# Grouped-query attention: row sums of the probabilities from a column of ones in the value matmuls, in place of running sums on POOL

## The chip, the cores and the metric

The kernel runs on one core of a Trainium2 chip. The metric is the device time of one execution in microseconds. The engines are named as in the profile: PE is the matrix engine (PEld its loads of weights), DVE the vector engine, ACT the scalar engine, POOL the general-purpose engine, SP the engine that issues most DMAs.

## The reference, cut to what matters

The program is a two-layer backbone over 1024 latent tokens and 256 context tokens of width 1024. The change lies in the even layer's mixer, where one half of the width is grouped-query attention: 8 query heads of 64 share 2 key and value heads. Latent queries attend to all 1280 tokens, context queries to the 256 of the context. The part that is computed differently is the softmax and what is multiplied with the values:

```python
def gqa_attend(q, keys, vals):
    ...
    def one(qblk):
        s = jnp.einsum('bqkgd,bskd->bkgqs', qblk, keys).astype(jnp.float32) * hd ** -0.5
        pr = jax.nn.softmax(s, axis=-1).astype(vals.dtype)
        return jnp.einsum('bkgqs,bskd->bqkgd', pr, vals)
```

## The kernel before

The kernel holds a float32 number as two parts, `hi` (rounded to the matrix engine's fast 32-bit form) and `lo` (what is left), made by `split`: ACT writes `hi` as a copy (L94), DVE writes `lo` as a subtraction (L95). A product is then two or three matmuls that add up in PSUM.

**The projection stage** (`in_proj0`, about 40 to 300 us). For each of the 10 token tiles of 128 (2 of context, 8 latent) `prep_kv` takes the projected keys and values. The values of the two heads are split into `v_st` (128 tokens, 2 heads, `hi` and `lo` of 64 columns) and stored by a DMA on SP to `gv` in DRAM (L505). `v_st` has one buffer. Then come the norm of the keys (`hr_ss`, `rs_t`), their rotation (`rp_u`, `rp_o`) and, one or two steps later, the transposes `kt_ps` on PE. Beside this runs `ada_halves`, which multiplies modulation weights (`w_ada`) on DVE into `ada_acc`.

**The attention stage** (`gqa`, about 300 to 668 us). A unit is one tile of 128 queries and one key head, hence 4 query heads, 512 columns side by side. There are 16 units of latent tiles, each over 10 key blocks of 128 tokens, and 4 of context tiles, each over 2: 168 key blocks in all. One unit's maxima are found while the unit before is computed: `score` (L731) makes scores by query rows, DVE reduces them to `gq_mx` (L732), then to `gq_m` and the negated `gq_mr` (L737), and `maxima` turns these into a row of 512 by four small matmuls `m_ps` (L743). For each key block, `front` makes the transposed scores `st_ps` with two matmuls (L751, L752; the second carries the maxima as an extra row), ACT takes the exponential into `gq_p` (L754), and `split` makes `gq_hi` and `gq_lo`. POOL adds `gq_p` into a running sum `gq_acc` for the unit: nothing at the first key block, L762 at the second, L765 at each further one. Two steps later `back` multiplies with the values: the weights are the 64 `hi` and 64 `lo` columns of the value head, and two matmuls with `gq_hi` (L772) and `gq_lo` (L773) as moving data add into `o_ps`. Rows 0 to 63 of `o_ps` then hold the product with the `hi` values, rows 64 to 127 that with the `lo` values.

At a unit's end `out` copies `o_ps` to SBUF (`o_sb`, L778) and `finish` takes the row sums: four transposes of `gq_acc` on PE (`l_ps`, L788, in one of the two PSUM banks that the scores `st_ps` use), a reduction of the 128 key rows on DVE (`gq_rl`, L789) and a reciprocal (L790). Four transposes of `o_sb` (`ot_ps`, L798) bring the result back to query rows, ACT and DVE add the two halves (L800, L801), and DVE scales by the reciprocal (L802).

The stages of one key block are written one behind the other, and `pipelined` interleaves successive blocks. `weave` mixes in `side0`, other work in fixed proportion: the remaining projection columns (`vg_ps`, L680 to L682, until about 625 us) and then the Hyena filters of the next layer (`tap_ps`, `hy_h`). On top of the written order a scheduler places the instructions of each engine by its own estimate of readiness; each engine then runs its row in that order.

Of the kernel before, what the change touches and what calls it, by code (L numbers as in the profile page):

```python
# [8 lines left out]
F32 = mybir.dt.float32  # L9
FR = mybir.dt.float32r  # L10
U32 = mybir.dt.uint32
ACTF = mybir.ActivationFunctionType
ALU = mybir.AluOpType
AX = mybir.AxisListType
# [9 lines left out]
NT = NC_T + NX_T  # L24
# [12 lines left out]
def f(ap):  # L37
    return ap.bitcast(F32)
# [43 lines left out]
def psa(g, shape, dt=F32, name="pa", tag="tr"):  # L82
    if tag not in g.ps_bufs:
        tag = "ac" if tag == "hy" and 0 and "ac" in g.ps_bufs else "sx"
    return g.ps.tile(shape, dt, name=name, tag=tag, bufs=g.ps_bufs[tag])
# [6 lines left out]
def split(g, hi, lo, src, pool=False):  # L92

    g.nc.scalar.activation(hi, src, ACTF.Copy)  # L94
    (g.nc.gpsimd if pool else g.nc.vector).tensor_tensor(lo, src, f(hi), op=ALU.subtract)  # L95
# [369 lines left out]
def in_proj0(g, ps, ftp, vgp):  # L465

    nc = g.nc
    src = (g.i["ctx"][0], g.i["x"][0])  # L470
    g.p0 = [g.dram.tile([128, GQA_Q], F32, name=f"p0_{t}") for t in range(NT)]
    g.gq = [g.dram.tile([128, 8, 128], F32, name=f"gq_{t}") for t in range(NT)]
    g.gk = g.dram.tile([128, 4, NT * 128], F32, name="gk")
    g.gv = g.dram.tile([128, NT, 256], F32, name="gv")
    w = g.i["ev_w_in"][0]
    ft = FeatT(g, ftp, ftp.tile([128, KT, 2, 256], FR, name="ftc", tag="ftc"))
    with ExitStack() as st:
        stg = st.enter_context(g.tc.tile_pool(name="ip_stg", bufs=3, reuse_waits="tile"))
        pr = st.enter_context(g.tc.tile_pool(name="ip_pr", bufs=1, reuse_waits="tile"))
        pq = []  # L480

        def head_norm(src, nh, gain):
            r = head_rstd(g, pq[0], src, nh, 64, f"rp_u{nh}")
            nc.vector.tensor_tensor(src, src, r.unsqueeze(2).to_broadcast([128, nh, 64]), op=ALU.mult)
            nc.gpsimd.tensor_tensor(src, src, gain.unsqueeze(1).to_broadcast([128, nh, 64]), op=ALU.mult)
# [13 lines left out]
        def prep_kv(t, ps):  # L499
            st = pq[0].tile([128, 288], F32, name="stg", tag="stgq", bufs=3)  # L500
            nc.scalar.copy(st, ps)
            nc.scalar.dma_start(out=g.p0[t][:, 1536:1568], in_=st[:, 0:32])
            vs = pq[0].tile([128, 2, 2, 64], FR, name="v_st", tag="v_st")
            split(g, vs[:, :, 0, :], vs[:, :, 1, :], st[:, 160:288].rearrange("p (h d) -> p h d", d=64))
            nc.sync.dma_start(out=g.gv[:, t, :], in_=f(vs).rearrange("p h w d -> p (h w d)"))  # L505
            src = st[:, 32:160].rearrange("p (h d) -> p h d", d=64)
            head_norm(src, 2, gk)
            return t, src
# [183 lines left out]
def gqa(g, y_put):  # L692


    nc = g.nc
    with ExitStack() as st:
        kv = st.enter_context(g.tc.tile_pool(name="gq_kv", bufs=1, reuse_waits="tile"))
        pr = st.enter_context(g.tc.tile_pool(name="gq_pr", bufs=2, reuse_waits="tile"))
        units = [(t, h) for t in range(NC_T, NT) for h in range(2)]
        ctx_units = [(t, h) for t in range(NC_T) for h in range(2)]  # L700
        qs, mx, sums, outs = {}, {}, {}, {}

        def load_q(u):
            t, h = u
# [5 lines left out]

        k1 = kv.tile([128, 2, NT * 128], FR, name="gq_k1")
        k2 = kv.tile([65, 2, NT * 128], FR, name="gq_k2")
        v = kv.tile([128, NT, 2, 2, 64], FR, name="gq_v")
        gk = g.gk.rearrange("p (h w) t -> p h w t", w=2)
        nc.sync.dma_start(out=f(k1), in_=gk[:, :, 0, :])
        load_q(units[0])
# [1 line left out]
        ones = kv.tile([128, 1], F32, name="gq_one")  # L718
        nc.vector.memset(ones, 1.0)
        for h in range(2):  # L720
            nc.vector.tensor_copy(k2[64:65, h, :], ones[64:65].to_broadcast([1, NT * 128]))
        nc.sync.dma_start(out=f(v).rearrange("p t h w d -> p t (h w d)"), in_=g.gv)

        def score(u, i):
            t, h = u
# [20 lines left out]
        def front(u, kt, nk):  # L746
            h = u[1]
            q1, q2 = (x.rearrange("p a b -> p (a b)") for x in qs[u])
            ks = slice(kt * 128, kt * 128 + 128)
            ps = psa(g, [128, 512], name="st_ps", tag="sk")  # L750
            nc.tensor.matmul(ps, k1[:, h, ks], q1, start=True, stop=False)  # L751
            nc.tensor.matmul(ps, k2[:, h, ks], q2, start=False, stop=True)  # L752
            p = pr.tile([128, 512], F32, name="gq_p", bufs=3)
            nc.scalar.activation(p, ps, ACTF.Exp, scale=0.125)  # L754
            hi = pr.tile([128, 512], FR, name="gq_hi", bufs=2 + 1)
            lo = pr.tile([128, 512], FR, name="gq_lo", bufs=2 + 1)
            split(g, hi, lo, p)
            if kt == 0:
                sums[u] = p
            elif kt == 1:  # L760
                acc = pr.tile([128, 512], F32, name="gq_acc")
                nc.gpsimd.tensor_tensor(acc, sums[u], p, op=ALU.add)  # L762
                sums[u] = acc
            else:
                nc.gpsimd.tensor_tensor(sums[u], sums[u], p, op=ALU.add)  # L765
            return u, kt, nk, hi, lo

        def back(u, kt, nk, hi, lo):
            if kt == 0:
                outs[u] = psa(g, [128, 512], name="o_ps", tag="o")  # L770
            vl = v[:, kt, u[1]].rearrange("p a d -> p (a d)")
            nc.tensor.matmul(outs[u], vl, hi, start=(kt == 0), stop=False)  # L772
            nc.tensor.matmul(outs[u], vl, lo, start=False, stop=(kt == nk - 1))  # L773
            return u,

# [4 lines left out]

        def finish(u, o_sb):
            t, h = u
            acc = sums.pop(u)
            rl = g.small.tile([128, 4], F32, name="gq_rl")
            if 1:
                ps = psa(g, [128, 4, 128], name="l_ps", tag=["tr", "ac", "sk", "sx"][2])
                for i in range(4):
                    nc.tensor.transpose(ps[:, i, :], acc[:, i * 128:(i + 1) * 128], g.ident)  # L788
                nc.vector.tensor_reduce(rl, ps, axis=AX.X, op=ALU.add)  # L789
                nc.vector.reciprocal(rl, rl)  # L790
            else:
                ps = psa(g, [128, 4], name="l_ps")
                for i in range(4):
                    nc.tensor.matmul(ps[:, i:i + 1], acc[:, i * 128:(i + 1) * 128], ones, start=True, stop=True)
                nc.vector.reciprocal(rl, ps)
            ps = psa(g, [128, 4, 128], name="ot_ps")
            for i in range(4):
                nc.tensor.transpose(ps[:, i, :], o_sb[:, i * 128:(i + 1) * 128], g.ident)  # L798
            y = pr.tile([128, 2, 4, 64], F32, name="gq_y")
            nc.scalar.copy(y[:, 0], ps[:, :, 64:128])  # L800
            nc.vector.tensor_tensor(y[:, 0], ps[:, :, 0:64], y[:, 0], op=ALU.add)  # L801
            nc.vector.tensor_tensor(y[:, 1], y[:, 0], rl.unsqueeze(2).to_broadcast([128, 4, 64]), op=ALU.mult)  # L802
            y_put(t, h * 256, y[:, 1].rearrange("p h d -> p (h d)"))

        def item(u, kt, nk):
# [1579 lines left out]
def tile_kernel(ctx, tc, ins, out):  # L2385
# [17 lines left out]
    with ExitStack() as sp:  # L2403
        banks(g, sp, "ps_d0", tr=2, ac=2, pb=2)
        hy_hidden(g)
        vg = in_proj0(g, sp, ftp, lambda: pool_of(s0, "vg", "right"))
# [195 lines left out]
```

## Time and profile before

| | |
|---|---|
| three runs, median (lowest to highest) | 3425.45 us (3423.26 to 3429.85) |
| the profiled execution's own time | 3425.51 us |
| its span in the trace | 3423.7 us |
| granted clock of PE over the span | 0.962 |
| busy, share of the span: PE, PEld | 91%, 70% |
| busy, share of the span: DVE, ACT, POOL | 75%, 45%, 22% |
| instructions on POOL over the span | 540 |

The span is what the trace covers; the 1.8 us between it and the execution's own time lie around it. PE's busy share counts each matmul from its start to its modelled end, and matmuls overlap, so a busy PE need not be one that takes a new matmul as soon as it could. A wait names the instruction whose end released the one that waited.

### The profile page before, as it was taken

How to read it: one execution, taken by the hardware profiler on the slowest of the kernel's cores; microseconds unless marked ns; L12 is line 12 of the kernel's file. 1: busy time of each engine (PE TensorE's matmuls, PEld its weight loads, DVE VectorE, ACT ScalarE, POOL GpSimd, SP SyncE). 2: the span in 40 equal slices, each digit the busy share in tenths (PEclk: the TensorE clock that was granted, in tenths of full speed). 3: DMA queues.
4: the chain of work that ended last, by engine and by line, in shares of the span. 5: the costliest groups of instructions: out<-in, count | busy, mean ns of one | idle time of the engine just before them, and what ended most of it. 6: DMA issues, size and time to landing. Idle time of an engine off the chain costs nothing.

```text
span 3423.7 us, 42030 instructions
## 1 busy us (share of the span) xinstructions
PE 3129.8 (91%) x13808; PEld 2402.8 (70%) x13808; DVE 2570.6 (75%) x4506; ACT 1538.5 (45%) x3150; POOL 736.5 (22%) x540
## 2 busy tenths in 40 slices
PE   8878999888987999989998899999968989999998
PEld 4765677567765788878877677776634667887886
DVE  6788898968748767666778757577788489876777
ACT  4444666645556222223345543576621352224443
POOL 0254555523322122200110112100011112210000
PEclk9999999899998999999999899999989999999999
DMA  6534111477753433468767445533344635438964
GB/s 227 152 122 148 48 44 44 117 221 212 259 201 110 142 133 132 148 218 298 255 227 230 167 151 166 131 88 77 125 133 147 209 112 183 142 139 296 313 197 156
DMA packets 344583, 566.69 MB, mean 166 GB/s; under 512 B 43329, under 2 KB 138561, under 8 KB 344236
## 3 DMA queue, kind: packets, MB, share of 16 engines
q1 hardware_dynamic: 296244, 491.17, 44.0%
q10 hardware_dynamic: 40952, 47.67, 4.1%
q0 software_dynamic: 7168, 25.17, 2.6%
q8 instruction: 109, 1.79, 0.2%
q14 instruction: 110, 0.90, 0.1%
HBM read 410.35 MB, written 153.54 MB: 165 GB/s over the span
## 4 chain that ended last, share of the span: by engine, by line
PE 56%; DVE 21%; issue 8%; DMA 7%; ACT 4%; POOL 3%; SPq 0%; ACTq 0%; POOLq 0%; DVEq 0%
PE up_ps L105 5%; PE up_ps L104 5%; PE up_ps L103 5%; PE dn_ps L1527 5%; PE dn_ps L1526 5%; PE dn_ps L1528 5%; DVE gq_lo L95 2%; DVE gq_mx L732 2%; PE s_ps L637 2%; PE up_ps L1245 1%; PE o_ps L2235 1%; DVE ada_acc L261 1%; DMA dn_b<-in_w_mlp_out 1%; PE pj_ps L104 1%; PE pj_ps L103 1%
## 5 line engine op out<-in xcount | busy, mean ns | idle before, releaser
L1526 PE MATMUL dn_ps<-dn_w_hi,dn_h_hi 128*128 128x512 f32 x896 | 352.9, 396 | 30.4 <-DVE accy L1507 16.1
L1527 PE MATMUL dn_ps<-dn_w_lo,dn_h_hi 128*128 128x512 f32 x896 | 354.1, 395 | 5.7 <-DVE dn_w_lo L95 5.5
L1528 PE MATMUL dn_ps<-dn_w_hi,dn_h_lo 128*128 128x512 f32 x896 | 352.7, 394 | 0.0
L95 POOL TENSOR_TENSOR w_lo<-up_w,w_hi 128x512 fp32r<-128x512 f32 x106 | 146.1, 1388 | 582.9 <-ACT w_hi L94 582.8
L94 ACT ACTIVATE dn_h_hi<-dn_h 128x512 fp32r<-128x512 f32 x224 | 140.8, 629 | 278.5 <-PE dn_ps L1527 196.4
L95 DVE TENSOR_TENSOR dn_h_lo<-dn_h,dn_h_hi 128x512 fp32r<-128x512 f32 x224 | 161.7, 722 | 79.7 <-ACT dn_h_hi L94 79.3
L1526 PEld LDWEIGHTS dn_ps<-dn_w_hi,dn_h_hi 128*128 128x128 f32 x896 | 170.4, 190 | 70.5 <-DVE accy L1507 17.7
L765 POOL TENSOR_TENSOR gq_acc<-gq_acc,gq_p 128x512 f32<-128x512 f32 x128 | 183.7, 1435 | 88.8 <-ACT gq_p L754 85.5
L1527 PEld LDWEIGHTS dn_ps<-dn_w_lo,dn_h_hi 128*128 128x128 f32 x896 | 171.0, 191 | 45.2 <-DVE dn_w_lo L95 9.8
L1528 PEld LDWEIGHTS dn_ps<-dn_w_hi,dn_h_lo 128*128 128x128 f32 x896 | 170.7, 190 | 35.5
L95 DVE TENSOR_TENSOR gq_lo<-gq_p,gq_hi 128x512 fp32r<-128x512 f32 x168 | 176.0, 1059 | 19.8 <-ACT gq_hi L94 19.5
L261 DVE SCALAR_TENSOR_TENSOR ada_acc<-w_ada,sc,ada_acc 128x512 f32<-128x512 f32 x224 | 170.6, 799 | 22.3 <-DMA w_ada<-in_w_ada 21.6
L95 POOL TENSOR_TENSOR ada_hl<-ada_acc,ada_hl 128x512 fp32r<-128x512 f32 x32 | 64.0, 2013 | 514.2 <-ACT ada_hl L94 362.5
L94 ACT ACTIVATE s_hi<-up_w 128x512 fp32r<-128x512 f32 x128 | 79.3, 630 | 190.4 <-DVE up_w L1234 116.3
L105 PE MATMUL up_ps<-t_hi,s_lo 128*128 128x512 f32 x384 | 152.7, 399 | 2.6 <-DVE s_lo L95 2.6
L104 PE MATMUL up_ps<-t_lo,s_hi 128*128 128x512 f32 x384 | 152.7, 398 | 1.9 <-DVE t_lo L95 1.9
L103 PE MATMUL up_ps<-t_hi,s_hi 128*128 128x512 f32 x384 | 153.1, 399 | 1.4 <-ACT t_hi L94 1.3
L1234 DVE TENSOR_TENSOR up_w<-up_w 128x512 f32<-128x512 f32 x128 | 94.0, 737 | 78.7 <-POOL w_lo L95 76.9
L647 DVE TENSOR_REDUCE sm_m<-s_ps 128x1 f32<-128x512 f32 (+1 forms) x192 | 110.5, 597 | 45.6 <-PE s_ps L637 44.3
L754 ACT ACTIVATE gq_p<-st_ps 128x512 f32<-128x512 f32 x168 | 99.5, 596 | 74.3 <-PE st_ps L752 57.0
L661 ACT ACTIVATE df_p<-s_ps,sm_m 128x512 f32<-128x512 f32 (+1 forms) x192 | 116.8, 619 | 34.5 <-DVE sm_m L651 31.2
L94 ACT ACTIVATE w_hi<-up_w 128x512 fp32r<-128x512 f32 x106 | 64.7, 629 | 145.1 <-DMA up_w<-in_w_mlp_in 65.1
(500 smaller groups left out, 9033.5 us busy)
## 6 DMA issues: line engine op xcount, KB each, us to landing
dn_b<-in_w_mlp_out SPq DMA_DIRECT2D x252, 256.0 KB
w_ada<-in_w_ada SPq DMA_DIRECT2D x96, 512.0 KB
up_w<-in_w_mlp_in SPq DMA_DIRECT2D x32, 1024.0 KB
hy_m<-in_k_ff POOLq DMA_DIRECT2D x32, 512.0 KB, 5.1
dn_c<-hidc SPq DMA_DIRECT2D x64, 256.0 KB
x<-x_in SPq DMA_DIRECT2D x26, 512.0 KB
x_in<-x SPq DMA_DIRECT2D x26, 512.0 KB
cb_raw<-in_od_w_in SPq DMA_DIRECT2D x20, 512.0 KB
```

The lines of the kernel that those rows point to most:

```text
L94: g.nc.scalar.activation(hi, src, ACTF.Copy)
L95: (g.nc.gpsimd if pool else g.nc.vector).tensor_tensor(lo, src, f(hi), op=ALU.subtract)
L103: nc.tensor.matmul(out, ah, bh, start=(i == 0), stop=False)
L104: nc.tensor.matmul(out, ah, bl, start=False, stop=False)
L105: nc.tensor.matmul(out, al, bh, start=False, stop=(i == n - 1))
L261: nc.vector.scalar_tensor_tensor(acc[:, s], w[:, k], sc, acc[:, s], op0=ALU.mult, op1=ALU.add)
L647: nc.vector.tensor_reduce(m[:, i:i + 1], s, axis=AX.X, op=ALU.max)
L661: g.nc.scalar.activation(d, s, ACTF.Exp, bias=m, scale=0.125, accum_out=l[:, i:i + 1])
L765: nc.gpsimd.tensor_tensor(sums[u], sums[u], p, op=ALU.add)
L1526: nc.tensor.matmul(ps, hh[:, sl], wh, start=(k == 0), stop=False)
L1527: nc.tensor.matmul(ps, hh[:, sl], wl, start=False, stop=False)
L1528: nc.tensor.matmul(ps, hl[:, sl], wh, start=False, stop=(k == nb - 1))
```

## The change

In the projection, `v_st` becomes 129 columns for each head: the 64 `hi` columns, one column of ones, the `lo` parts of columns 1 to 63, and last the `lo` part of column 0. The split becomes the copy on ACT, two subtractions and one copy of ones on DVE. `gv` and `gq_v` hold 258 numbers per token in place of 256.

In the attention the matmuls of `back` take columns 0 to 127 as weights. Row 64 of `o_ps` then sums the probabilities themselves. The missing `lo` column 0 gets a matmul of its own for each key block, with one column of weights and `gq_hi` as moving data, which adds into row 0 of `o_ps`. The additions on POOL, the transposes `l_ps` and the reduction L789 are gone; the reciprocal is taken from column 64 of the transposed result, and the addition of the halves covers columns 1 to 63.

```diff
-    g.gv = g.dram.tile([128, NT, 256], F32, name="gv")
+    g.gv = g.dram.tile([128, NT, 258], F32, name="gv")
...
+        ones = pr.tile([128, 1, 1], F32, name="v_one")
+        nc.vector.memset(ones, 1.0)
...
-            vs = pq[0].tile([128, 2, 2, 64], FR, name="v_st", tag="v_st")
-            split(g, vs[:, :, 0, :], vs[:, :, 1, :], st[:, 160:288].rearrange("p (h d) -> p h d", d=64))
-            nc.sync.dma_start(out=g.gv[:, t, :], in_=f(vs).rearrange("p h w d -> p (h w d)"))
+            vs = pq[0].tile([128, 2, 129], FR, name="v_st", tag="v_st")
+            vr = st[:, 160:288].rearrange("p (h d) -> p h d", d=64)
+            nc.scalar.activation(vs[:, :, 0:64], vr, ACTF.Copy)
+            for d0, d1, c0 in ((1, 64, 65), (0, 1, 128)):
+                nc.vector.tensor_tensor(vs[:, :, c0:c0 + d1 - d0], vr[:, :, d0:d1], f(vs[:, :, d0:d1]), op=ALU.subtract)
+            nc.vector.tensor_copy(vs[:, :, 64:65], ones.to_broadcast([128, 2, 1]))
+            nc.sync.dma_start(out=g.gv[:, t, :], in_=f(vs).rearrange("p h d -> p (h d)"))
...
-        v = kv.tile([128, NT, 2, 2, 64], FR, name="gq_v")
+        v = kv.tile([128, NT, 2, 129], FR, name="gq_v")
...
-            if kt == 0:
-                sums[u] = p
-            elif kt == 1:
-                acc = pr.tile([128, 512], F32, name="gq_acc")
-                nc.gpsimd.tensor_tensor(acc, sums[u], p, op=ALU.add)
-                sums[u] = acc
-            else:
-                nc.gpsimd.tensor_tensor(sums[u], sums[u], p, op=ALU.add)
...
-            vl = v[:, kt, u[1]].rearrange("p a d -> p (a d)")
+            vl = v[:, kt, u[1], 0:128]
             nc.tensor.matmul(outs[u], vl, hi, start=(kt == 0), stop=False)
+            nc.tensor.matmul(outs[u][0:1], v[:, kt, u[1], 128:129], hi, start=False, stop=False)
             nc.tensor.matmul(outs[u], vl, lo, start=False, stop=(kt == nk - 1))
...
-                for i in range(4):
-                    nc.tensor.transpose(ps[:, i, :], acc[:, i * 128:(i + 1) * 128], g.ident)
-                nc.vector.tensor_reduce(rl, ps, axis=AX.X, op=ALU.add)
-                nc.vector.reciprocal(rl, rl)
...
-            nc.scalar.copy(y[:, 0], ps[:, :, 64:128])
-            nc.vector.tensor_tensor(y[:, 0], ps[:, :, 0:64], y[:, 0], op=ALU.add)
-            nc.vector.tensor_tensor(y[:, 1], y[:, 0], rl.unsqueeze(2).to_broadcast([128, 4, 64]), op=ALU.mult)
+            nc.vector.reciprocal(rl, ps[:, :, 64:65])
+            nc.scalar.copy(y[:, 0], ps[:, :, 0:64])
+            nc.vector.tensor_tensor(y[:, 0, :, 1:64], ps[:, :, 65:128], y[:, 0, :, 1:64], op=ALU.add)
+            nc.vector.tensor_tensor(y[:, 1], y[:, 0], rl.to_broadcast([128, 4, 64]), op=ALU.mult)
```

Because a scheduler places the instructions, their order changes with the edit, from the value split to shortly behind the attention stage; before and behind that the rows of PE are the same. Three places follow, each as it stands in the two programs. Names with a number are buffers (`q_5149` is a query tile of the unit, `q_5432` one of the next).

PE, at the end of a latent unit in the middle of the stage, before: each key block has two value matmuls, and at the unit's end stand the two sets of four transposes.

```order
L751 MATMUL st_ps<-q_5149,gq_k_2721 128x512
L752 MATMUL st_ps<-q_5150,gq_k_2722 128x512
L772 MATMUL o_ps<-gq_hi,gq_v 128x512
L773 MATMUL o_ps<-gq_lo,gq_v 128x512
L788 MATMUL l_ps<-ident,gq_acc 128x128 x4
L798 MATMUL ot_ps<-ident,o_sb 128x128 x4
L751 MATMUL st_ps<-q_5149,gq_k_2721 128x512
L752 MATMUL st_ps<-q_5150,gq_k_2722 128x512
L772 MATMUL o_ps<-gq_hi,gq_v 128x512
L773 MATMUL o_ps<-gq_lo,gq_v 128x512
```

And after, at the corresponding place (line numbers shift by a few):

```order
L758 MATMUL st_ps<-q_5103,gq_k_2743 128x512
L759 MATMUL st_ps<-q_5104,gq_k_2744 128x512
L771 MATMUL o_ps<-gq_hi,gq_v 128x512
L772 MATMUL o_ps<-gq_hi,gq_v 1x512
L773 MATMUL o_ps<-gq_lo,gq_v 128x512
L786 MATMUL ot_ps<-ident,o_sb 128x128 x4
L758 MATMUL st_ps<-q_5103,gq_k_2743 128x512
L759 MATMUL st_ps<-q_5104,gq_k_2744 128x512
L771 MATMUL o_ps<-gq_hi,gq_v 128x512
L772 MATMUL o_ps<-gq_hi,gq_v 1x512
L773 MATMUL o_ps<-gq_lo,gq_v 128x512
```

One set of transposes is gone, and each key block has a third matmul, 1x512, between the `gq_hi` and the `gq_lo` one.

POOL, at the passage from the projection to the attention, before (`ada_hl` belongs to the modulation, `rp_u` and `rp_o` to the rotation of queries):

```order
L609 TENSOR_TENSOR rp_u<-stg,tq_328 128x256 x2
L611 TENSOR_TENSOR rp_o<-rp_o,rp_u 128x512
L95 TENSOR_TENSOR ada_hl<-ada_acc,ada_hl 128x512 x2
L762 TENSOR_TENSOR gq_acc<-gq_p 128x512
L765 TENSOR_TENSOR gq_acc<-gq_acc,gq_p 128x512 x8
```

And after (`qblk`, `vblk` and `ab` are buffers of the stage behind the attention, set to zero):

```order
L616 TENSOR_TENSOR rp_u<-stg,tq_330 128x256 x2
L618 TENSOR_TENSOR rp_o<-rp_o,rp_u 128x512
L95 TENSOR_TENSOR ada_hl<-ada_acc,ada_hl 128x512 x2
L875 MEMSET qblk_6590 128x1024
L875 MEMSET vblk_6591 128x1024
L875 MEMSET ab_6592 128x1024
```

Between the last work of the projection and the buffers of the next stage POOL has nothing left to do.

DVE, in the projection around one tile's value split, before:

```order
L118 SCALAR_TENSOR_TENSOR rs_t<-rs_t 128x2
L261 SCALAR_TENSOR_TENSOR ada_acc<-w_ada,sc,ada_acc 128x512
L484 TENSOR_TENSOR stg<-stg,rs_t 128x128
L95 TENSOR_TENSOR v_st<-stg,v_st 128x2x64
L113 TENSOR_SCALAR rs_t<-hr_ss 128x2
L604 TENSOR_TENSOR rp_o<-stg,tq_327 128x128
L261 SCALAR_TENSOR_TENSOR ada_acc<-w_ada,sc,ada_acc 128x512 x2
L116 SCALAR_TENSOR_TENSOR rs_t<-rs_t 128x2
```

And after:

```order
L261 SCALAR_TENSOR_TENSOR ada_acc<-w_ada,sc,ada_acc 128x512
L511 CAST v_st<-v_one 128x2
L116 SCALAR_TENSOR_TENSOR rs_t<-rs_t 128x2
L510 TENSOR_TENSOR v_st<-stg,v_st 128x2x63
L510 TENSOR_TENSOR v_st<-stg,v_st 128x2
L117 TENSOR_TENSOR rs_t<-rs_t 128x2
L261 SCALAR_TENSOR_TENSOR ada_acc<-w_ada,sc,ada_acc 128x512
L118 SCALAR_TENSOR_TENSOR rs_t<-rs_t 128x2
L261 SCALAR_TENSOR_TENSOR ada_acc<-w_ada,sc,ada_acc 128x512
L487 TENSOR_TENSOR stg<-stg,rs_t 128x128
L261 SCALAR_TENSOR_TENSOR ada_acc<-w_ada,sc,ada_acc 128x512
```

One row on `v_st` has become three, spread between the norm of the keys and the `ada_acc` operations. On SP, two of the ten stores of `v_st` also stand one `w_ada` load later than before.

## Rows read from the trace of the kernel before

**Rows 1.** Windows: stretch, length, busy per engine (instructions), PE's granted clock, DMA share, GB/s.
```profile
309.00:668.00 359.00, 321.31 (x1442) 240.67 (x1441) 329.86 (x501) 239.31 (x419) 217.28 (x157) 0.97 0.17 53
120.00:290.00 170.00, 136.83 (x698) 110.00 (x697) 137.94 (x275) 68.28 (x176) 83.90 (x80) 0.91 0.50 154
...
418.30:441.40 23.10, 19.63 (x85) 13.53 (x84) 22.32 (x33) 15.22 (x28) 15.37 (x10) 1.00 0.07 23
...
576.20:597.10 20.90, 20.34 (x96) 16.08 (x95) 19.65 (x30) 13.95 (x26) 12.78 (x9) 1.00 0.12 39
...
645.60:666.20 20.60, 15.38 (x55) 9.53 (x53) 20.57 (x26) 12.41 (x25) 12.31 (x8) 0.84 0.35 96
...
632.30:635.70 3.40, 3.14 (x11) 2.59 (x12) 3.40 (x9) 2.20 (x4) 3.40 (x4) 0.50 0.05 10
639.10:642.50 3.40, 3.30 (x9) 2.57 (x10) 3.29 (x7) 2.80 (x6) 2.08 (x3) 0.51 1.01 260
659.60:669.90 10.30, 8.21 (x21) 5.29 (x22) 9.08 (x14) 3.35 (x6) 3.48 (x3) 0.50 0.20 59
```

**Rows 2.** Waits of PE from 309 to 668: total us, times, longest.
```profile
PE o_ps L773 <- DVE gq_lo L95: 18.3, 28, 1.9
PE m_ps L743 <- DVE gq_mr L737: 11.5, 12, 2.0
PE s_ps L731 <- DVE gq_mx L732: 2.3, 3, 0.9
PE m_ps L743 <- DVE gq_mx L732: 1.8, 1, 1.8
PE tap_ps L1905 <- DVE w_lo L95: 1.3, 1, 1.3
PE st_ps L751 <- DVE gq_rl L789: 0.9, 1, 0.9
```

**Rows 3.** Timeline of PE at a unit's end: start, us, instruction.
```profile
490.53 0.39 PE L773 MATMUL o_ps<-gq_lo,gq_v 128*128 128x512 f32 x1
...
490.76 0.60 PE L788 MATMUL l_ps<-ident,gq_acc 128*128 128x128 f32 x4
...
491.20 0.60 PE L798 MATMUL ot_ps<-ident,o_sb 128*128 128x128 f32 x4
```

**Rows 4.** Page, costliest groups: busy us, mean ns, idle before and releaser.
```profile
L95 DVE TENSOR_TENSOR dn_h_lo<-dn_h,dn_h_hi 128x512 fp32r<-128x512 f32 x224 | 161.7, 722 | 79.7 <-ACT dn_h_hi L94 79.3
...
L95 DVE TENSOR_TENSOR gq_lo<-gq_p,gq_hi 128x512 fp32r<-128x512 f32 x168 | 176.0, 1059 | 19.8 <-ACT gq_hi L94 19.5
```

**Rows 5.** Timeline of POOL and DVE in the attention stage.
```profile
483.90 1.28 POOL L765 TENSOR_TENSOR gq_acc<-gq_acc,gq_p 128x512 f32<-128x512 f32 x1 [1.95 <-ACT gq_p L754]
...
484.45 1.28 DVE L95 TENSOR_TENSOR gq_lo<-gq_p,gq_hi 128x512 fp32r<-128x512 f32 x1 [1.89 <-ACT gq_hi L94]
...
486.67 0.68 DVE L95 TENSOR_TENSOR gq_lo<-gq_p,gq_hi 128x512 fp32r<-128x512 f32 x1
```

**Rows 6.** Groups by line, 309 to 668: busy us, mean ns, idle before.
```profile
L789 DVE TENSOR_REDUCE gq_rl<-l_ps 128x4 f32<-128x512 f32 x20 | 13.6, 678 | 0.3 <-PE l_ps L788 0.3
...
L737 DVE TENSOR_SCALAR gq_mr<-gq_m 128x4 fp32r<-128x4 f32 x19 | 12.4, 654 | 0.3
```

**Rows 7.** Groups by line, 120 to 180, DVE in the projection.
```profile
L95 DVE TENSOR_TENSOR v_st<-stg,v_st 128x128 fp32r<-128x128 f32 x10 | 3.3, 326 | 1.6 <-ACT v_st L94 1.6
...
L118 DVE SCALAR_TENSOR_TENSOR rs_t<-rs_t 128x2 f32<-128x2 f32 x9 | 1.4, 153 | 0.0
```

**Rows 8.** Timeline of PE and PEld around one-column matmuls of the modulation rows.
```profile
1767.29 0.39 PE L1539 MATMUL dc_ps<-dx_hi,dn_c 128*128 128x512 f32 x1
...
1767.52 0.63 PE L277 MATMUL ada_ps<-ada_hl,colsr 128*1 128x512 f32 x2
...
1767.75 0.19 PEld L1526 LDWEIGHTS dn_ps<-dn_w_hi,dn_h_hi 128*128 128x128 f32 x1 [0.15 <-issue]
...
1767.99 0.39 PE L1526 MATMUL dn_ps<-dn_w_hi,dn_h_hi 128*128 128x512 f32 x1
```

More of the change, by code (lines that the diff above doesn't have):

```diff
@@ L700, in gqa @@
         ctx_units = [(t, h) for t in range(NC_T) for h in range(2)]
-        qs, mx, sums, outs = {}, {}, {}, {}
+        qs, mx, outs = {}, {}, {}
         def load_q(u):
@@ L721, in gqa @@
             nc.vector.tensor_copy(k2[64:65, h, :], ones[64:65].to_broadcast([1, NT * 128]))
-        nc.sync.dma_start(out=f(v).rearrange("p t h w d -> p t (h w d)"), in_=g.gv)
+        nc.sync.dma_start(out=f(v).rearrange("p t h d -> p t (h d)"), in_=g.gv)
         def score(u, i):
@@ L782, in finish @@
             t, h = u
[L783 to L786, printed above, removed]
-                for i in range(4):
-                    nc.tensor.transpose(ps[:, i, :], acc[:, i * 128:(i + 1) * 128], g.ident)
-                nc.vector.tensor_reduce(rl, ps, axis=AX.X, op=ALU.add)
-                nc.vector.reciprocal(rl, rl)
[L791 to L795, printed above, removed]
+            rl = g.small.tile([128, 4, 1], F32, name="gq_rl")
             ps = psa(g, [128, 4, 128], name="ot_ps")
```

## The prediction

> **What bounds the kernel now.** I read the windows first, one for the whole attention stage (309 to 668 us) and one for each of its units, then the waits of PE, the timeline where two engines meet, and the groups by line.
>
> The stage is 359 us long; PE is busy for 321.31 of it, DVE for 329.86, ACT for 239.31, POOL for 217.28 [rows 1]. So two engines are close to full, and which of them sets the pace changes from unit to unit. In the unit from 418.3 to 441.4 DVE works 22.32 of 23.10 us and PE only 19.63; in the last unit DVE works 20.57 of 20.60 and PE 15.38; in the unit from 576.2 to 597.1 PE works 20.34 of 20.90 [rows 1]. The waits of PE say the same: it stood 18.3 us in 28 places for `gq_lo`, 11.5 and 1.8 us in 13 places for the maxima, and 2.3, 1.3 and 0.9 us in 5 more for other results of DVE [rows 2]. That is 36.1 us in 46 gaps, all behind DVE. A matmul lasts 0.39 us but the next starts 0.23 us behind it [rows 3], so each gap hides another 0.16 us of an array that drains and still counts as busy: 46 x 0.16 = 7.4 us. PE thus loses 43.5 us to DVE, say 45 with the gaps too short to be seen.
>
> Why DVE is full is in two more views. The 168 `gq_lo` subtractions average 1059 ns; the same operation on the same shape in the down projection averages 722 [rows 4]. The timeline shows the mechanism: a POOL addition runs from 483.90 to 485.18; a `gq_lo` that starts under it at 484.45 takes 1.28 us, which is 0.73 until POOL has ended and 0.55 behind that; the next one, with POOL idle, takes 0.68 [rows 5]. While POOL adds, DVE's subtraction of two SBUF tiles stands.
>
> **The change part by part.**
>
> *POOL's 148 additions go* (16 units of 10 key blocks with nine each, 4 of 2 with one). Nobody waits long for POOL itself, but `gq_lo` should fall from 1.06 to about 0.70 us, between the undisturbed 0.68 [rows 5] and the 722 ns [rows 4]: 168 x 0.36 = 60 us off DVE. `gq_mr`, a 128x4 operation, takes 654 ns on average [rows 6] though a 128x2 one takes 153 elsewhere [rows 7]: another 19 x 0.5 = 9.5 us.
>
> *The turn of the row sums goes*: on PE 20 sets of four transposes of `gq_acc`, 0.44 us from the start of one set to what follows [rows 3], 8.8 us; on DVE 20 reductions of 678 ns, 13.6 us [rows 6]. The reciprocal that stays reads four columns of PSUM instead of SBUF, and the addition of the two halves covers 63 columns of 64: nothing. `l_ps` shared its two banks with the score tiles; PE's 0.9 us for `gq_rl` [rows 2] is in the 45 already.
>
> DVE's sum in the stage is then 329.86 - 60 - 9.5 - 13.6 = 247 us of 359, and with ACT unchanged at 239 neither can set the pace. PE is what is late next.
>
> *168 matmuls of one column by 512 come to PE.* This stage has none, but the modulation rows have: one column of weights, 512 moving columns, two in a row. They start at 1767.52, their neighbour before at 1767.29, the one behind at 1767.99 [rows 8]: 0.23 us to get in, 0.235 for each. That is the price of a 128-column matmul: 168 x 0.235 = 39.5 us onto PE. The lower bound by these rows is 0.23 each, 38.6; the upper is twice that for those that fall in a stretch at half clock (about 0.50 in three places [rows 1]).
>
> The Trainium skill speaks against this part: the page "TensorEngine Tiling (Array Packing)", section Key Properties, says that changing the tiling mode, not just the tile, drains TensorE, and a one-column matmul might run in a smaller mode than its full neighbours. The trace does not agree so far: rows 8 show no drain on either side. By the trace the term is 39.5 us; by the page it would be the sum of the fourth rival.
>
> *What remains of the 45 us.* The unit that PE already paces, 576.2 to 597.1, shows it: 0.56 us without PE work [rows 1]. I take 0.55 us for each ten key blocks; 168 blocks make 9 us, so 36 us of waiting go. Bounds: all 45 go, or half stay, since the matmul of the maxima waits for a chain through PE and DVE that merely gets shorter. The new matmul helps: it stands between the `gq_hi` and the `gq_lo` matmul, so `gq_lo` has 0.23 us more before PE asks for it.
>
> *The clock.* PE's granted clock is 0.50, which is 1.2 of 2.4 GHz, for 3.4, 3.4 and 10.3 us near the end of the stage [rows 1], behind the long waits of its last units. With PE busier I expect it to fall later or not at all. Half of these 17.1 us, 8.5, is what there is to win, and some of it lies behind the stage; I take 5, with bounds of 0 and 8.5.
>
> *The split of the values grows.* For each of 10 token tiles one subtraction of 326 ns [rows 7] becomes one of 63 columns a head, one of a single column a head, and a copy of the ones. The two small ones I price by the 128x2 row, 153 ns [rows 7]: 10 x 2 x 0.15 = 3 us on DVE. From 120 to 290 us DVE has 32 of 170 us free [rows 1], so between 0 and 3 shows, 5 if they meet POOL's operations there. The store of `v_st` waits for all three, and behind it on SP stand loads of `w_ada`; on DVE `rs_t` and `hr_ss` stand behind them, and PE's `kt_ps` transposes in the end. The instructions there also stand in another order, which can give or take some us. I take +2. The memset of ones and 8 bytes more in each 1024 of `gv` are nothing beside the loads. The value weights now begin at odd words (129 a head); no row shows such a load of weights, but it has 0.23 us for its 0.19 [rows 8] under the matmul before, so I take zero; 0.1 us more for each would cost 336 x 0.06 = 20 us.
>
> **The sum**, against the profiled execution's own 3425.51 us (the median of the runs is 3425.45, no shift): -8.8 + 39.5 - 36 - 5 + 2 = -8.3, so 3417. It is a small difference of large terms: 31 us of work onto PE, 41 us of waiting and slow clock off it.
>
> **The rivals.**
>
> *All waits go.* DVE would have a third of its time free, so perhaps even the maxima are never late: -8.8 + 39.5 - 45 - 8.5 + 1 = -21.8, 3404. For it: DVE at 247 us. Against: score, maximum, negation, `m_ps` and its copy are a serial chain.
>
> *The waits stay and PE pays: slower.* If PE's waits are an affair of its order and of the chains rather than of DVE's load, half of them remain and no clock comes back: -8.8 + 39.5 - 23 + 2 = +9.7, 3435. Without the clock's 5 us the kernel is slower from 45 - 32.7 = 12 us of remaining waits on, with them from 17. For it: units that PE paces already have hardly a wait to give, and pay 10 x 0.235 - 0.44 = 1.9 us each. Against: 36 of the 37.7 us in which PE idles name DVE [rows 1, 2].
>
> *POOL is not what slows DVE.* Then only 13.6 us leave DVE, it stays at 316 of 359, and at most as much of the waits goes: -8.8 + 39.5 - 13.6 + 2 = +19, 3445. Against it: rows 5.
>
> *The array drains around each one-column matmul.* A drain costs 0.16 us, the part of a matmul that the next one overlaps [rows 3], twice for each of 168: 54 us on the forecast, 3471. Rows 8 speak against it. It is the rule of the Trainium skill's page "TensorEngine Tiling (Array Packing)" named above.
>
> *The gain is lost behind the stage.* The filters that run beside the last unit go on behind it; if their chain through DVE and DMA sets the start of the next stage, the 8 us are waited for there: 3425. Against: they are issued as the stage's own loop advances, so they start earlier too.
>
> **How the numbers follow.** A measurement of this kernel can tell about 0.2%, 6.9 us, from no change. Chances: the forecast, with 5 to 17 us of remaining waits, 0.60, of which 0.38 lies more than 6.9 us below and 0.22 within; all waits go 0.14, faster; lost behind 0.10, same; waits stay 0.10, of which 0.08 is slower and 0.02 within; POOL not the cause 0.03 and drains 0.03, slower. Together faster 0.52, same 0.34, slower 0.14. The range of 3404 to 3433 leaves out the drains, the case of POOL, most of the waits that stay, and half of the case in which all go: under 0.2.
>
> **What would show it.** In the changed stage `gq_lo` averages 680 to 730 ns; DVE is busy some 250 us and PE over 0.95 of the time; the one-column matmuls stand 0.23 us from their neighbours; PE's waits for DVE sum to 5 to 17 us; the clock stays at 1.00 up to the last unit; the stage takes 345 to 355 us in place of 359. Wrong would be: `gq_lo` still near 1 us, more than 0.3 us around the new matmul, a half clock as long as before, or 120 to 290 us longer by more than 5.

## The result and the profile after

The changed kernel takes **3391.02 us** (median of 4 runs, 3387.06 to 3396.04) against 3424.59 (3423.26 to 3429.85, with one run more of the kernel before than its first table has): a ratio of 0.990, 95% interval 0.9887 to 0.9913. Two copies of it gave 0.9904 (0.9886 to 0.9922) and 0.9898 (0.9882 to 0.9915). The forecast of 3417 had the sign; the lower end of its range, 3404 to 3433, is 13 us above the median.

The page of the changed kernel, busy time by engine:

```profile
PE 3134.7 (93%) x13896; PEld 2405.3 (71%) x13896; DVE 2489.5 (74%) x4507; ACT 1538.6 (45%) x3150; POOL 528.0 (16%) x392
```

Windows of the changed kernel, columns as in [rows 1]: the attention stage, then the projection ahead of it.

```profile
308.20:642.90 334.70, 329.51 (x1536) 245.56 (x1534) 248.46 (x489) 242.07 (x421) 7.24 (x9) 1.00 0.19 56
120.00:290.00 170.00, 138.34 (x705) 111.81 (x704) 143.13 (x297) 69.55 (x177) 89.87 (x80) 0.90 0.52 161
```

Beside the first row of [rows 1]: the stage is 334.70 us long where it was 359 to 361 (the chosen edges differ by 2 us), though PE is counted busy for 8 us more. DVE fell from 329.86 to 248.46 us, the 247 of the forecast; the granted clock is 1.00 where it was 0.97. What PE idles in the stage fell from 37.7 to 5.2 us. In the projection DVE rose by 5.2 us and the stage began at 308.2 instead of 309.0, so nothing of that showed.

The waits of PE in that stage (columns as in [rows 2]), all that the trace lists:

```profile
PE tap_ps L1894 <- ACT w_hi L94: 1.4, 1, 1.4
PE m_ps L750 <- DVE gq_mr L744: 1.1, 1, 1.1
PE st_ps L759 <- ACT q L751: 1.0, 2, 0.7
PE ot_ps L786 <- ACT o_sb L778: 0.7, 1, 0.7
PE o_ps L771 <- ACT o_sb L778: 0.4, 1, 0.4
```

Of the 36.1 us behind DVE in [rows 2], 1.1 us is left, in one gap. (The listed waits sum to 4.6 of the 5.2 us; the rest are gaps too short to be listed.) The groups of DVE in the stage (out and in, count, busy us, mean ns, idle before):

```profile
L95 DVE TENSOR_TENSOR gq_lo<-gq_p,gq_hi 128x512 fp32r<-128x512 f32 x168 | 115.4, 690 | 55.9 <-ACT gq_hi L94 54.3
L739 DVE TENSOR_REDUCE gq_mx<-s_ps 128x1 f32<-128x256 f32 (+1 forms) x196 | 105.7, 579 | 21.6 <-PE s_ps L738 20.9
L791 DVE TENSOR_TENSOR gq_y<-gq_y,gq_rl 128x256 f32<-128x256 f32 x20 | 8.4, 419 | 0.3
...
L744 DVE TENSOR_SCALAR gq_mr<-gq_m 128x4 fp32r<-128x4 f32 x19 | 4.1, 218 | 0.4
L95 DVE TENSOR_TENSOR w_lo<-w_raw,w_hi 128x1024 fp32r<-128x1024 f32 x3 | 3.7, 1223 | 1.0 <-ACT w_hi L94 1.0
```

`gq_lo` went from 1059 ns [rows 4] to 690, `gq_mr` from 654 [rows 6] to 218. But for that one gap DVE now waits for ACT and PE, and PE not for it.

A key block in the timeline of the changed kernel (start, us, engine, line, operation):

```profile
480.42 0.39 PE L758 MATMUL st_ps<-q,gq_k 128*128 128x512 f32 x1
480.64 0.39 PE L759 MATMUL st_ps<-q,gq_k 65*128 65x512 f32 x1
480.87 0.40 PE L771 MATMUL o_ps<-gq_hi,gq_v 128*128 128x512 f32 x1
481.11 0.40 PE L772 MATMUL o_ps<-gq_hi,gq_v 128*1 128x512 f32 x1
481.34 0.40 PE L773 MATMUL o_ps<-gq_lo,gq_v 128*128 128x512 f32 x1
481.58 0.39 PE L687 MATMUL vg_ps<-w_hi,ftx_hi 128*128 128x512 f32 x1
```

The one-column matmul at 481.11 stands 0.24 us behind its neighbour and 0.23 ahead of the next, as in [rows 3, 8]. No drain shows.

**Where the time went**, profiled execution against profiled execution (3423.7 to 3385.3 us of span, 38.4): 0.8 ahead of the attention, 26.2 in it (360.9 to 334.7, first `gq_p` to last `gq_y`), 11.4 behind it (2753.8 to 2742.4). The profiled run of the changed kernel was the lowest of its four, 4 us under their median; between medians the gain is 33.6 us.

### The profile page after: what moved, and what is told of

The parts are those of the page before. It is cut to its first block, busy times and chain, and to the rows that moved or that the text cites. A ratio compares the mean times of both kernels' runs of the same rounds, so it can differ in the third digit from the quotient of the medians.

```text
span 3385.3 us, 41884 instructions
## 1 busy us (share of the span) xinstructions
PE 3134.7 (93%) x13896; PEld 2405.3 (71%) x13896; DVE 2489.5 (74%) x4507; ACT 1538.6 (45%) x3150; POOL 528.0 (16%) x392
## 4 chain that ended last, share of the span: by engine, by line
PE 63%; DVE 14%; issue 10%; DMA 7%; ACT 3%; POOL 3%; SPq 0%; ACTq 0%; POOLq 0%; DVEq 0%
PE up_ps L105 5%; PE up_ps L104 5%; PE up_ps L103 5%; PE dn_ps L1516 5%; PE dn_ps L1515 5%; PE dn_ps L1517 5%; PE s_ps L644 2%; PE up_ps L1234 1%; PE s_ps L738 1%; PE o_ps L2224 1%; DMA up_w<-in_w_mlp_in 1%; PE st_ps L758 1%; PE st_ps L759 1%; DVE ada_acc L261 1%; PE o_ps L771 1%
## 5 line engine op out<-in xcount | busy, mean ns | idle before, releaser
L1515 PEld LDWEIGHTS dn_ps<-dn_w_hi,dn_h_hi 128*128 128x128 f32 x896 | 169.8, 190 | 67.7 <-DVE accy L1496 16.1
L95 DVE TENSOR_TENSOR gq_lo<-gq_p,gq_hi 128x512 fp32r<-128x512 f32 x168 | 115.4, 690 | 55.9 <-ACT gq_hi L94 54.3
L739 DVE TENSOR_REDUCE gq_mx<-s_ps 128x1 f32<-128x256 f32 (+1 forms) x208 | 112.2, 580 | 29.1 <-PE s_ps L738 28.2
```

What stands on the lines that cost most here:

```text
L739: nc.vector.tensor_reduce(mx[u][:, i, j:j + 1], ps, axis=AX.X, op=ALU.max)
L1515: nc.tensor.matmul(ps, hh[:, sl], wh, start=(k == 0), stop=False)
```

## The experiments

| kernel | median us | ratio (95%) | attention stage us | behind it us |
|---|---|---|---|---|
| changed | 3391.02 | 0.990 (0.9887 to 0.9913) | 334.7 | 2742.4 |
| e1_no_adds | 3374.25 | 0.9845 (0.9831 to 0.986) | 307.4 | 2758.3 |
| e2_adds_back | 3422.79 | 0.9992 (0.9981 to 1.0002) | 367.8 | 2743.8 |
| e3_no_column | 3363.21 | 0.9814 (0.9798 to 0.9831) | 300.9 | 2752.5 |
| e4_pool_fill | 3396.18 | 0.9914 (0.9899 to 0.9929) | 337.7 | 2749.4 |
| before_again | 3425.85 | 1.0002 (0.9992 to 1.0013) | 363.1 | 2755.9 |
| after_again | 3393.01 | 0.9904 (0.9886 to 0.9922) | 334.8 | 2750.1 |
| e5_wide_rows | 3422.86 | 0.9995 (0.9985 to 1.0005) | 362.5 | 2751.3 |
| e6_ones_in_sbuf | 3386.68 | 0.9886 (0.9872 to 0.9901) | 334.4 | 2744.1 |
| e7_column_twice | 3425.8 | 1.0003 (0.9993 to 1.0014) | 370.7 | 2744.4 |
| after_third | 3390.69 | 0.9898 (0.9882 to 0.9915) | 335.2 | 2744.2 |
| e6_again | 3391.62 | 0.9905 (0.9889 to 0.9921) | 333.2 | 2745.5 |

The theory: POOL's additions slow DVE, DVE makes PE wait, and the one-column matmul costs PE one ordinary slot. The rivals: the waits went for another reason (the turn of the sums, the new matmul, the order); the one-column matmul costs something else; what lies behind the stage moved for reasons of its own.

### e1_no_adds: the kernel before, without POOL's additions

```diff
+        flat = kv.tile([128, 512], F32, name="gq_flat")
+        nc.vector.memset(flat, 1.0)
...
-            if kt == 0:
-                sums[u] = p
-            elif kt == 1:
...
-                nc.gpsimd.tensor_tensor(sums[u], sums[u], p, op=ALU.add)
+            sums[u] = flat
```

`flat` is a constant tile, so the division by the sums is left out; transposes and reductions of `l_ps` stay.

> The kernel before, without POOL's 148 additions; the turn of the sums stays, but turns a constant tile, so the division by the row sums is left out of what is computed. Theory (POOL's additions hold up DVE's subtraction, and DVE's lateness was nearly all of PE's idle time): gq_lo falls to about 0.69 us, PE's waits for DVE nearly vanish, and against the changed kernel (3391 us) PE has 39 us of one-column matmuls less and 9 us of transposes more, so about 3361, 3355 to 3370. Rival 1 (the gain came from the turn of the sums and the other order, not from POOL's additions): 3410 or more. Rival 2 (the one-column matmuls cost nothing, they hide): about 3391.

The window of its attention stage:

```profile
308.80:616.20 307.40, 303.99 (x1448) 239.12 (x1446) 254.00 (x504) 237.28 (x421) 7.24 (x9) 1.00 0.20 62
```

All waits of PE behind DVE in it, and the group of `gq_lo`:

```profile
PE o_ps L768 <- DVE gq_lo L95: 0.8, 3, 0.4
...
PE m_ps L745 <- DVE gq_mr L739: 0.2, 1, 0.2
...
L95 DVE TENSOR_TENSOR gq_lo<-gq_p,gq_hi 128x512 fp32r<-128x512 f32 x168 | 114.0, 687 | 38.5 <-ACT gq_hi L94 35.6 <-PE o_ps L768 1.8
```

With the additions alone gone, `gq_lo` falls to 687 ns, the waits behind DVE fall from 36.1 to 1.0 us, the clock is 1.00, and the stage is 53.5 us shorter, with the turn of the sums and its 20 reductions still there. So the waits were POOL's doing; neither the turn nor the new matmul was needed to take them away. The total came 13 us above the 3361 expected, and 4 above the upper end: the stage is 27.3 us shorter than the changed kernel's, but behind it this kernel takes 2758.3 us, as the kernel before does.

### e2_adds_back: the changed kernel, with the additions put back

```diff
             split(g, hi, lo, p)
+            if kt == 0:
+                sums[u] = p
...
+                nc.gpsimd.tensor_tensor(sums[u], sums[u], p, op=ALU.add)
             return u, kt, nk, hi, lo
```

Nobody reads the sums; the columns of ones stay in use.

> The changed kernel with POOL's 148 additions put back beside it; nobody reads their sums. Theory: gq_lo is back at about 1.05 us, DVE at some 320 us of the attention stage, PE's waits for gq_lo and the maxima return, and PE still pays for the new matmuls: 3420 to 3440. Rival 1 (the additions did not matter): 3391 to 3397. A case between would say that the matmul between the two value matmuls covers part of the lateness.

The window of its stage:

```profile
307.80:675.60 367.80, 340.60 (x1534) 246.40 (x1533) 323.95 (x490) 242.07 (x419) 216.99 (x157) 0.98 0.17 51
```

PE's waits behind DVE in it:

```profile
PE m_ps L750 <- DVE gq_mr L744: 11.0, 9, 2.4
PE o_ps L781 <- DVE gq_lo L95: 11.0, 12, 2.1
PE m_ps L750 <- DVE gq_lo L95: 2.1, 1, 2.1
PE s_ps L738 <- DVE gq_mx L739: 1.7, 3, 1.0
```

And the group of `gq_lo`:

```profile
L95 DVE TENSOR_TENSOR gq_lo<-gq_p,gq_hi 128x512 fp32r<-128x512 f32 x168 | 176.1, 1056 | 27.0 <-ACT gq_hi L94 26.1
```

It held. `gq_lo` is back at 1056 ns, PE waits 25.8 us for DVE, and the kernel is as slow as the one before (its stage is 6.9 us longer, what lies behind it 10 us shorter). Put beside e1, the change has two parts: taking the additions away is worth 53.5 us of the stage of the kernel before, the rest of the change then costs 27.3 (307.4 to 334.7). The parts do not simply add. With the additions still there the rest costs only 6.9 us (360.9 to 367.8), because PE does part of its new work in time in which it had waited for DVE (36.1 us of such waits become 25.8); taking the additions away after that is worth 33.1 (367.8 to 334.7).

### e3_no_column: the changed kernel, without the one-column matmuls

```diff
-            nc.tensor.matmul(outs[u][0:1], v[:, kt, u[1], 128:129], hi, start=False, stop=False)
```

This leaves out the low part of one value column of 64 in each head.

> The changed kernel without the 168 one-column matmuls; the low part of one value column in 64 is left out of what is computed. Theory (PE paces the stage and each of these costs its 0.23 us): 39 us less, about 3352, up to 3362 if ACT or DVE come to pace single units. Rival 2 (they hide in gaps of PE): 3380 to 3391.

The window of its stage:

```profile
307.90:608.80 300.90, 295.38 (x1367) 232.56 (x1366) 243.95 (x490) 234.28 (x420) 7.25 (x9) 0.99 0.21 63
```

The waits of PE that have come up in it:

```profile
PE o_ps L772 <- DVE gq_lo L95: 1.1, 3, 0.6
PE o_ps L771 <- ACT o_sb L777: 0.8, 1, 0.8
PE st_ps L758 <- ACT gq_p L761: 0.7, 1, 0.7
```

Only 33.8 us of the stage went, 0.20 for each of the 168, and 28 us of the total; I had expected 39. To see why, I summed over the stage, for each line and shape, the matmuls times their median distance from start to start (0.233 us for L772). These slots fall from 327.2 us to 287.8, what 168 slots are worth; what of the stage lies beyond the slots rises from 7.5 to 13.2 us. PE came nearer to DVE and ACT: the matmuls that start over 0.1 us behind their slot rise from 17 to 45. Of the 5.7 us more, the records of the clock account for 1.7 (3.4 us at a granted clock of 0.50, where the changed kernel has none). That left two readings, the full slot or 0.20 us, for e7.

### e4_pool_fill: POOL writes instead of adding

```diff
             split(g, hi, lo, p)
+            if kt:
+                fill = pr.tile([128, 1024], F32, name="gq_fill", bufs=1)
+                nc.gpsimd.tensor_tensor(fill[:, 0:1], p[:, 0:1], p[:, 1:2], op=ALU.add)
+                nc.gpsimd.memset(fill, 0.0)
```

> The changed kernel with POOL kept busy beside each key block but the first of a unit, by a memset of 128x1024 (0.95 us in the kernel before) behind a 128x1 addition that reads the probabilities: POOL writes SBUF but hardly reads it. If it is POOL's reading that holds up DVE: gq_lo stays near 0.70 us and the time at 3391 to 3397. If any POOL work on SBUF does: gq_lo at 0.85 us or more, and 3400 to 3420.

The window of its stage:

```profile
307.40:645.10 337.70, 331.29 (x1536) 246.70 (x1534) 250.68 (x489) 242.68 (x421) 186.79 (x305) 0.99 0.18 56
```

Two rows of its timeline:

```profile
481.74 0.95 POOL L768 MEMSET gq_fill<- 128x1024 f32 x1
481.90 0.69 DVE L95 TENSOR_TENSOR gq_lo<-gq_p,gq_hi 128x512 fp32r<-128x512 f32 x1 [0.46 <-ACT gq_hi L94]
```

The group of `gq_lo`:

```profile
L95 DVE TENSOR_TENSOR gq_lo<-gq_p,gq_hi 128x512 fp32r<-128x512 f32 x168 | 116.7, 698 | 58.7 <-ACT gq_hi L94 56.4
```

POOL is busy for 186.79 us, against 217 with the additions, and `gq_lo` averages 698 ns. The subtraction at 481.90 lies wholly under POOL's memset and takes 0.69 us; the one under an addition took 1.28 [rows 5]. So a busy POOL does not hold up this subtraction; one that reads as it adds does. Nor did the additions cost much by keeping `gq_p`: in the whole stage of the kernel before, ACT waited 2.8 us for POOL to be done with it. By the Trainium skill, page "SBUF — State Buffer", section Who interferes with whom, a DVE instruction with two SBUF inputs contends with a GpSimd instruction that reads SBUF and not with one that only writes. The trace agrees: 1056 ns with reads (e2), 698 with writes and a 128x1 addition, 690 with an idle POOL.

It is otherwise with `gq_mr`, which has one input in SBUF and four columns, and takes 0.17 us by its median. Where it starts under a memset, it ends with it: five times in e4 it ends 0.03 us behind a memset (0.34 to 0.44 us, and 2.37 us under three in a row). The last wait of PE behind DVE in the changed kernel, 1.1 us, is of this kind; the memsets are those of the next stage's buffers:

```profile
611.27 0.95 POOL L875 MEMSET vblk<- 128x1024 f32 x1
611.99 1.15 DVE L744 TENSOR_SCALAR gq_mr<-gq_m 128x4 fp32r<-128x4 f32 x1
612.17 0.95 POOL L875 MEMSET ab<- 128x1024 f32 x1
...
613.29 0.40 PE L750 MATMUL m_ps<-identr,gq_mr 128*1 128x128 f32 x4
```

The stage of e4 is 3.0 us longer than that of the changed kernel; the longest wait of PE in it is new, 2.4 us for a DMA (`w_raw`).

### before_again and after_again: what one trace is worth

Copies of the two kernels, for the 11 us behind the stage.

> A copy of the kernel before, for a second trace. If the 11 us that the changed kernel's first trace gained behind the attention stage are chance of one execution, the times of the later stages (first up projection 484.4, first down projection 508.1, differential attention 538.5, the rest 734.3 us in the first trace) scatter here by 3 to 6 us each. If they are not chance, each comes back within 1.5 us.

> A copy of the changed kernel, for a second trace and a second ratio. Time 3387 to 3396. The attention stage 334 to 336 us under every theory. If the gain behind the stage is the kernel's own, the later stages come back as 482, 502.4, 536 and 732.6 us within 1.5 us each (sum 2253); if it was chance of one execution, their sum comes nearer to the 2265 us of the kernel before.

The stages of the kernel before came back as 484.5, 508.1, 538.4 and 734.5 us, within 0.2 of the first trace. Those of the changed kernel came back as 482.2, 504.8, 537.8 and 735.3, in sum 2260 where the first trace had 2253: neither answer. A third trace has 479.1, 501.8, 537.7 and 735.4. So the gain behind the stage is 4 to 13 us, by the pair of traces that one takes; what the last two stages gave in the first trace was that execution's, and only the two projections (2.2 to 5.4 us the first, 3.3 to 6.3 the second) gain in every pair.

### e5_wide_rows and e6_ones_in_sbuf: is it the place of the scratch arrays?

The first widens only the DRAM rows of `gv` in the kernel before (its store and its load take the first 256); the second brings the changed kernel back to the old DRAM layout. Of each edit the main lines:

```diff
-    g.gv = g.dram.tile([128, NT, 256], F32, name="gv")
+    g.gv = g.dram.tile([128, NT, 258], F32, name="gv")
...
```

```diff
...
-        nc.sync.dma_start(out=f(v).rearrange("p t h d -> p t (h d)"), in_=g.gv)
+        nc.sync.dma_start(out=f(v)[:, :, :, 0:128], in_=g.gv.rearrange("p t (h d) -> p t h d", h=2))
+        nc.vector.tensor_copy(v[:, :, :, 128:129], ones.unsqueeze(1).unsqueeze(1).to_broadcast([128, NT, 2, 1]))
...
```

(The columns of a head are then low part of the first value column, high parts, other low parts, one.)

> The kernel before, with the rows of gv in DRAM 258 wide in place of 256 (two words of padding, never read), so that everything allocated behind gv in DRAM stands 10,240 bytes further on, as in the changed kernel. Theory A, the gain behind the attention stage comes from where the scratch arrays lie: the attention stage stays at 361 us, the later stages take 11 us less, time 3411 to 3417. Theory B, it comes from what the stage itself leaves behind (clock, or the times at which transfers start): no change, 3422 to 3430.

> The changed kernel, but the column of ones is not sent through DRAM: gv is 256 wide again as in the kernel before (so all scratch arrays lie where they lay), and the ones are written into gq_v once, in the attention stage. The work of PE, DVE and ACT in the attention stage is that of the changed kernel but for one copy of 20 columns. Theory A (placement): attention stage 335 us, later stages as in the kernel before, so 11 us over the changed kernel, 3399 to 3405. Theory B: as the changed kernel, 3386 to 3396; ten copies fewer on DVE in the in-projection would give at most 2 us.

Both came out by theory B: 3422.86 and 3386.68 us. The place of the arrays is not the cause. The stage behind the attention in which the two groups of kernels differ most is the first down projection. Its window in the kernel before:

```profile
1506.50:2014.60 508.10, 481.63 (x2093) 388.17 (x2094) 368.07 (x620) 233.99 (x441) 55.99 (x21) 0.96 0.69 227
```

And in the changed kernel:

```profile
1476.60:1979.00 502.40, 479.06 (x2093) 387.16 (x2094) 367.21 (x620) 233.84 (x441) 55.97 (x21) 0.97 0.69 229
```

The same instructions on every engine, nearly the same busy time, and 5.7 us between them. As an estimate of what the clock takes I count half of the time that the trace records at a granted clock of 0.50 (1.2 of 2.4 GHz); where PE waits at that time, it is less. In this stage that is 18.6 of 508.1 and 20.3 of 508.1 us in the two traces of before, 16.6 of 506.1 in e5, 13.6 of 502.4, 15.0 of 504.8 and 16.1 of 501.8 in the three of the changed kernel, and 16.6 of 504.6 in e6. Without it the seven are 486 to 490 us. So by this estimate what differs there is mainly how much of the stage the chip spent at half clock. Over all traces the first down projection takes 506.1 to 509.2 us in the four of kernels built on the one before, and 501.8 to 505.4 in the nine of kernels built on the changed one, e2 among them, whose attention stage waits as before. What makes that difference of some 4 us is open.

### e7_column_twice: the price of the one-column matmul

```diff
             nc.tensor.matmul(outs[u][0:1], v[:, kt, u[1], 128:129], hi, start=False, stop=False)
+            nc.tensor.matmul(outs[u][0:1], v[:, kt, u[1], 128:129], hi, start=False, stop=False)
```

> The changed kernel with each one-column matmul issued twice (168 more; the second adds the low part of one value column once more, so that column's low part counts double). It prices the one-column matmul where PE sets the pace and nothing waits: leaving them out saved only 33.8 us of the stage. Theory A, each is worth a full slot of 0.230 us and the rest came back as waits when they were left out: stage 334.7 + 38.6 = 373 us (372 to 376), time 3426 to 3436. Theory B, one is really cheaper than its slot (0.20 us, the 33.8 us by 168): stage 368 to 369, time 3421 to 3427. If the clock falls in the longer stage, both are a few us more.

Its stage:

```profile
307.40:678.10 370.70, 367.75 (x1703) 259.80 (x1701) 251.49 (x489) 244.19 (x419) 7.24 (x9) 1.00 0.17 51
```

A key block in it:

```profile
481.21 0.39 PE L771 MATMUL o_ps<-gq_hi,gq_v 128*128 128x512 f32 x1
481.44 0.40 PE L772 MATMUL o_ps<-gq_hi,gq_v 128*1 128x512 f32 x1
481.68 0.40 PE L773 MATMUL o_ps<-gq_hi,gq_v 128*1 128x512 f32 x1
481.91 0.40 PE L774 MATMUL o_ps<-gq_lo,gq_v 128*128 128x512 f32 x1
```

36.0 us more than 334.7, between the two answers. The slots decide: the next matmul starts 0.233 us behind a one-column matmul (median of the 336), all slots of the stage sum to 364.4 us (327.2 and 168 x 0.233 = 39.1 would be 366.3), and what lies beyond them fell from 7.5 to 6.3. The price is 0.23 us on PE; what leaving one out or adding one moves the end by is 0.20 and 0.21, because a fuller PE waits less.

### after_third and e6_again: is the version without ones in DRAM faster?

> The changed kernel once more, as the partner of the next one on the same chip: 3387 to 3396, ratio to the kernel before 0.990. The stage 334 to 336 us; behind it anything from 2742 to 2752 us, with the difference in the granted clock.

> The version with the ones written in the attention stage once more, beside the changed kernel on the same chip. If its first ratio, 0.9886 against 0.9904, is its own, it is 3 to 7 us faster, of which 2 us come from the in-projection (305.9 against 307.6 and 308.2 us); if it was chance of some executions, the two medians lie within 3 us.

On the same chip the two have 3390.69 and 3391.62 us: no difference that can be told. The in-projection of the copy of e6 took 307.2 us, that of the changed kernel 307.3. So nothing is left of the first ratio that can be told from chance.

## Why the prediction missed, point by point

*The mechanism* was right in its links; what failed are sizes. POOL's additions hold up DVE's subtraction (e1, e2; not its writes, e4), `gq_lo` fell to 690 ns (forecast 680 to 730), DVE to 248.46 us (247), PE became the bound (busy 329.51 of 334.70 us), the one-column matmul costs an ordinary slot without a drain, the stage runs at full clock.

*The one-column matmuls*: 39.5 us forecast, 168 x 0.233 = 39.1 in the slots. Right. *The turn of the sums*: 8.8 forecast. Its 80 transposes follow one another at 0.109 us (median in before), 8.7 us. Right; e1 against e3, whose stages differ mainly in that turn, gives 307.4 - 300.9 = 6.5 us at the end of the stage.

*What remains of the 45 us* was the step that failed first. I let 36 go and 9 stay, by the 0.56 us in which PE idled in one unit of ten key blocks that PE already paced [rows 1], and took that for a floor of such a unit. All waits of PE in that unit (before, 576.2 to 597.1 us) are these:

```profile
PE o_ps L773 <- DVE gq_lo L95: 0.6, 2, 0.3
```

It was not a floor: both gaps stand behind `gq_lo`, which averages 1109 ns there, so they are the very delay that the change takes away. In the changed kernel 1.1 us of waits behind DVE remain in the whole stage, in e1, without the help of the new matmul, 1.0; PE's idle time of every cause is 5.2 us, 0.31 for ten key blocks. Counted in slots as in e3, the stage had 298.2 us of slots and 62.8 beyond them before, and has 327.2 and 7.5 now. So 55.3 us went, and with the 10.2 of the clock (next point) taken off the term was nearer -45. A wait seen under the load that the change takes away says nothing on what stays without it.

*The clock* was the second. I took 5 of what the half clock cost. The stage went from 0.97 to 1.00: by the estimate above it had lost 10.2 us (12.6 in the second trace), and now it loses none. My upper bound of 8.5 came from three stretches, 17.1 us; in all the stage has 20.4 us recorded at half clock. Half was a compromise between "later" and "not at all", although it hung on the same waits: where these go (the changed kernel, e1), all of it comes back, and where they return (e2), 7.5 us are lost again. The two terms were one, and belonged in one case.

With these two the stage is -8.8 + 39.5 - 45 - 10.2 = -24.5, against -26.2 measured; the other 2 us are slots, which rose by 29.0 us and not by 30.7. 334.7 us is below the 345 to 355 that I gave for it.

*The in-projection*: +2 forecast, -0.8 measured (307.3 to 308.2 us in three traces, against 309.0 and 308.2). DVE's 5.2 us more were covered, the lower end of what I gave.

*Behind the stage* I forecast nothing but the loss of the gain. It was not lost: 11.4 us more came, in this pair of traces 9.5 of them in the granted clock (by the estimate above 98.6 us lost to it behind the stage before, 89.1 after). That share does not repeat: the third trace of the changed kernel has 2744.2 us there, 9.6 less than before, and 97.0 lost to the clock. Part of the 11.4 was this execution, since the second trace has 2750.1; the rest came in every pair of traces, is not explained, and is about as large as what a measurement can tell. No row of the kernel before could have given it.

The misses sum up: 9 us of waits, 5 of clock and 2 of slots in the stage, 3 in the in-projection and 11 behind are the 30 us between 3417 and the 3387.06 of the profiled run.

*The rivals.* The one that came true is "all waits go". Its 3404 was high by 11 us that came behind the stage, 3 in the stage and 2 in the in-projection. It had 0.14 because score, maximum, `m_ps` and its copy are a serial chain; but that chain has the length of a unit to run in, and with DVE relieved it was late once: 0.2 us in e1, and 1.1 in the changed kernel, there behind a memset of POOL (e4). "The waits stay" is refuted by e1, "POOL is not what slows DVE" by e1 and e2, the drain by the timeline above and by e7. The rule of the Trainium skill's page "TensorEngine Tiling (Array Packing)", section Key Properties, is about a change of the tiling mode; whether a one-column matmul between full ones changes the mode, no run here shows. That it drains the array is not borne out: 0.23 us a slot with one (the changed kernel) or two in a row (e7).

## What to carry to other kernels

An addition on POOL is not free where DVE works on two SBUF tiles at the time: here 148 of them cost the stage 53.5 us in the kernel before and 33.1 beside the new matmuls, while the rest of the change, which does the same sums with full slots on TensorE, costs 27.3 once the additions are gone. When a change frees an engine that makes TensorE wait, the waits and the half clock that follows them are one term: in the stage of this kernel both went to next to nothing. And an idle time read under the old load is no floor for what stays under the new one: ask first behind what it stands.

## What the runs showed of the hardware that was not expected

- Not only `gq_lo` was slowed by POOL: with the additions gone the second `gq_y` operation went from 735 to 419 ns and the 128x1024 `w_lo` from 1951 to 1223, each with two SBUF inputs, and `gq_mr`, with one, from 654 to 218. The maxima, read from PSUM, stayed at 578 and 579. The rows of before that [rows 4, 6] do not have:

```profile
L802 DVE TENSOR_TENSOR gq_y<-gq_y,gq_rl 128x256 f32<-128x256 f32 x19 | 14.0, 735 | 0.2
...
L95 DVE TENSOR_TENSOR w_lo<-w_raw,w_hi 128x1024 fp32r<-128x1024 f32 x3 | 5.9, 1951 | 0.0
...
L732 DVE TENSOR_REDUCE gq_mx<-s_ps 128x1 f32<-128x256 f32 (+1 forms) x195 | 104.2, 578 | 7.4 <-PE s_ps L731 7.3
```

- A POOL that only writes for most of 186.79 us of the stage left `gq_lo` at 698 ns, but it holds `gq_mr`, which has one input, to the end of the memset under way: 2.37 us at the longest, against 0.17.
- The same 2093 matmuls of one stage took 501.8 to 509.2 us in different traces, and 486 to 490 when the time lost to half clock is taken off in the seven shown. A difference of 5 us in one stage between two single traces is no finding by itself.
